# A table of 200 steps: moving the second half of the side work between attention blocks

## The chip, the core and the metric

The kernel runs on one core of a Trainium2 chip. A core has TensorE (PE in the profile, matmuls, with PEld for its weight loads), VectorE (DVE), ScalarE (ACT), GpSimd (POOL) and SyncE (SP, which here only issues transfers). The engines run side by side and wait for each other by semaphores; each works through its own list in the order in which it was built. The metric is the device time of one execution in microseconds, the median over runs.

## The reference

A hybrid encoder block on 1024 tokens of width 1024, with 16 learned meta tokens ahead of them, all in float32:

```python
u = _rms_norm(h, pre_w)
rq, rk, rv, rg, aq, ak, av, ag, gr, ga = _split_in(u @ w_in)
...                       # branch A: o_r = bidirectional retention, 4 heads, gated by silu(rg)
y_r = o_r.astype(h.dtype) @ w_rb
aq = _pad_front(_rotary(aq.reshape(B, T, ATT_HEADS, ATT_HD), pos))     # 8 heads of 128
ak = _pad_front(_rotary(ak.reshape(B, T, ATT_GROUPS, ATT_HD), pos))    # 2 groups of keys
o_a = _windowed_sink_attention(aq, ak, av, sink)[:, META_PAD:].reshape(B, T, ATT_Q)
y_a = (o_a * jax.nn.silu(ag.astype(jnp.float32))).astype(h.dtype) @ w_ab
mix = jax.nn.sigmoid(gr) * y_r + jax.nn.sigmoid(ga) * y_a
return h + _rms_norm(mix @ w_o, post_w)
```

The attention works in blocks of 128 queries. Each sees its own block of keys, the ones beside it (distance at most 128) and the 16 meta keys; a learned sink per head enters the softmax's maximum and sum.

## The kernel before

Every float32 product is made of three fp32r products: each operand is split in a high and a low half (`...h`, `...l`), and `mm3` (L72) issues high x high (L74), low x high (L75) and high x low (L76). The high half of most operands is a copy on ACT, the low half is a subtraction on DVE (`dve_lo`, L90).

The program has four stretches: the first projections and retention (0 to about 337 us), the attention (about 337 to 570), the gates' and branches' products, and the output product with its norm. The change lies in the attention.

The attention takes the 8 heads in 4 pairs, hp = 0 to 3, and each pair in 8 blocks, n = 0 to 7: 32 chunks, written (hp, n), with k as their running number. For a chunk, `stage1` makes the scores of both heads on TensorE (`ps`), masks them and takes the row minimum on DVE (`raw`, `nm`, L1369), makes exponentials and their sum on ACT (`p`, `den`, L1372), the inverse on DVE (L1375) and the scaling on POOL (L1382). `stage2` transposes p on TensorE (`pt`) and splits the result (`pah`, `pm`, `pbh` on ACT; `pal`, `pm`, `pbl` on DVE). `stage3` multiplies by the values (`po`) and copies out on ACT (`oa`, L1440).

TensorE's order is: scores of the next chunk, transposes of this one, then `fill`: some steps of other matmuls, as many as `FILL` says (5 to 10), then `stage3` of the chunk before. A step is three matmuls of 512 columns and takes about 0.7 us: such matmuls start 0.235 us apart. There are 200 steps: projections of later queries (`gen_aq`, tile `paq`) and keys (`gen_ak`, `pak`), and the first part of later gate products (`pre`, `pe`). The queries of pair 3 take steps 128 to 159. The weight units of `pre` take eight steps each from 160: unit 9 at 160, 10 at 168, 11 at 176, 12 at 184, 13 at 192.

What else those steps need, on ACT, DVE and by transfers, is begun by the table `BEGUN`: step number, then the functions that are called right after it. They are:

- `sum_fetch(q)` loads, and `sum_row(q, 0)` and `(q, 1)` scale on ACT (L726) and subtract on DVE (L729) one eighth of the sums of x (tile `xs`, two operations on ACT and four on DVE in all), which are stored for products after the attention.
- `fetch_aq(hp)` loads a query weight; `half_w('q', hp, s)` splits its half s (`wh` on ACT L116, `wl` on DVE L90, both 128x1024).
- `split_q(hp, e, i)` splits rotated queries (`aqh` on ACT L641, `aql` on DVE L90): half i of the blocks of head e of the pair. The tiles are aq_00, 01, 10, 11, with i first.
- `keys(1, i)` splits the rotated keys `akr` of piece i (`kTh` on ACT L687, `kTl` on DVE L90). The rotation itself ends in two transfers that POOL issues (L185).
- `pre_fetch(u)` loads the two halves of a gate weight (`we`, L762; the two buffers are shared with the unit before), `pre_sum(u, 0..2)` makes sums in it on DVE (L774) and `pre_parts(u)` splits it (`weh` on ACT L784, `wel` on DVE L90).

`hooked` puts what it begins behind the latest mark of the attention, and a scheduler then sets the final order of each engine's list:

```python
with follow(*marks("exp", "sum", "lo", "hi")):
    for f, *a in at.get(n, ()):
        f(*a)
```

`x_to_out` copies 1 MB of x to the output, three times, after the chunks that a tuple names. It issues on SP, as do all loads and stores here but the rotations' (POOL).

Of the kernel before, what the change touches and what calls it, by code (L numbers as in the profile page):

```python
# [38 lines left out]
def block_kernel(ctx: ExitStack, tc: tile.TileContext, x0, xT, x, meta, w_in, w_rb, w_ab, w_out, post_w,  # L39
# [39 lines left out]
    def follow(*ins):  # L79

        st = ExitStack()
        for i in ins:
            st.enter_context(tc.issue_after(i))
        return st
# [595 lines left out]
    def keys(g, i):  # L680

        if not i:
            kT[g] = [ra.tile([P, 4, 272], R, tag="kp", bufs=2, name=f"kT{s}{g}") for s in "hl"]
        kh, kl = kT[g]
        o = rotated_k.pop((g, i))
        s = NM if i == 0 else 0
        nc.scalar.copy(kh[:, i, 0:256], o[:, s:s + 256])  # L687
        dve_lo(kl[:, i, 0:256], o[:, s:s + 256], kh[:, i, 0:256])
        if i == 0:
            for j in range(4):  # L690
                nc.scalar.copy(kh[:, j, 256:272], o[:, 0:NM])
                dve_lo(kl[:, j, 256:272], o[:, 0:NM], kh[:, j, 256:272])
# [139 lines left out]
    def marks(*names):  # L832
        return [last[m] for m in names if m in last]
# [498 lines left out]
    def attention():  # L1332
# [96 lines left out]
        def stage3(hp, n):  # L1429
            g = hp // 2  # L1430
            bl, m = st2.pop((hp, n))
            po = p3(f"po{hp}_{n}")
            for j, (b, h_, l_) in enumerate(bl):
                mm3(po[:, 0:256], *(t[:, P * g:P * g + P] for t in (vah[:, b], low_value(b))), h_, l_, j == 0, False)
            latest[:] = [nc.tensor.matmul(po[:, 0:256], vm[:, P * g:P * g + P], m, start=False,
                                          stop=True).ins]
            if n % 2 == 0:
                oa[0] = ap.tile([P, 2, 256], F32, tag="oa", bufs=2, name=f"oa{hp}_{n}")
            o0 = P * (n % 2)
            last["oa"] = nc.scalar.copy(oa[0][:, :, o0:o0 + P],  # L1440
                                        po[:, 0:256].rearrange("p (e t) -> p e t", e=2)).ins
            if n % 2:
                stored.append(nc.sync.dma_start(
                    oTa_d[2 * hp:2 * hp + 2, :, P * (n - 1):P * (n + 1)].rearrange("e p t -> p e t"), oa[0]).ins)
# [13 lines left out]
        for k, (hp, n) in enumerate(chunks):  # L1458
            ends = k >= len(chunks) - 2
            if k + 1 < len(chunks):  # L1460
                with follow(*latest, *marks("oa", "lo")):
                    stage1(*chunks[k + 1])
                if chunks[k + 1] == (1, NB - 1):
                    keys(1, 0)
            if chunks[k] == (3, NB - 2):

                with follow(*latest):
                    fill(FILL[hp][n])
                yield
            if not k:  # L1470
                with follow(*latest):
                    fill(FILL[hp][n] - 3)
            with follow(*latest, *marks("exp", "sum")) if not ends else ExitStack():
                stage2(hp, n)
            if k and not ends:
                with follow(*latest):
                    fill(FILL[hp][n])
            with follow(*latest) if not ends else ExitStack():
                if k:
                    stage3(*chunks[k - 1])  # L1480
            if ends:
                yield
            if k in (12, 17, 21):
                x_to_out({12: 0, 17: 4, 21: 6}[k])
        stage3(*chunks[-1])


# [4 lines left out]
             39: [(sum_fetch, 1)], 40: [(pre_sum, 8, 0)], 41: [(pre_sum, 8, 1)], 42: [(pre_sum, 8, 2)],  # L1492
             43: [(pre_parts, 8)], 44: [(fetch_aq, 2)], 48: [(sum_row, 1, 0)], 49: [(sum_row, 1, 1)],
             52: [(sum_fetch, 2)], 53: [(half_w, 'q', 2, 0)], 58: [(half_w, 'q', 2, 1)], 60: [(fetch_ak,)],
             61: [(split_q, 1, 0, 1)], 65: [(split_q, 1, 1, 1)], 68: [(half_w, 'k', 1, 0)],
             72: [(half_w, 'k', 1, 1)], 74: [(sum_row, 2, 0)], 75: [(sum_row, 2, 1)], 78: [(sum_fetch, 3)],
             82: [(split_q, 2, 0, 0)], 88: [(sum_row, 3, 0)], 89: [(sum_row, 3, 1)], 90: [(split_q, 2, 1, 0)],
             91: [(sum_fetch, 4)], 96: [(sum_row, 4, 0)], 97: [(sum_row, 4, 1)], 99: [(sum_fetch, 5)],
             104: [(keys, 1, 1)], 105: [(fetch_aq, 3)], 107: [(sum_row, 5, 0)], 108: [(sum_row, 5, 1)],
             110: [(sum_fetch, 6)], 112: [(split_q, 2, 0, 1)], 114: [(half_w, 'q', 3, 0)],  # L1500
             116: [(half_w, 'q', 3, 1)], 118: [(pre_fetch, 9)], 121: [(sum_row, 6, 0)], 122: [(sum_row, 6, 1)],
             123: [(keys, 1, 2)], 124: [(sum_fetch, 7)], 125: [(pre_sum, 9, 0)], 128: [(pre_sum, 9, 1)],
             129: [(split_q, 2, 1, 1)], 130: [(pre_sum, 9, 2)], 133: [(pre_parts, 9)], 134: [(pre_fetch, 10)],
             136: [(keys, 1, 3)], 139: [(sum_row, 7, 0)], 140: [(sum_row, 7, 1)], 145: [(split_q, 3, 0, 0)],
             146: [(pre_sum, 10, 0)], 147: [(pre_sum, 10, 1)], 149: [(pre_sum, 10, 2)], 152: [(split_q, 3, 1, 0)],
             153: [(pre_parts, 10)], 154: [(pre_fetch, 11)], 161: [(pre_sum, 11, 0)], 162: [(pre_sum, 11, 1)],
             163: [(pre_sum, 11, 2)], 164: [(split_q, 3, 0, 1)], 167: [(pre_parts, 11)], 168: [(pre_fetch, 12)],
             169: [(split_q, 3, 1, 1)], 173: [(pre_sum, 12, 0)], 174: [(pre_sum, 12, 1)], 175: [(pre_sum, 12, 2)],
             177: [(pre_parts, 12)], 178: [(pre_fetch, 13)], 182: [(pre_sum, 13, 0)], 183: [(pre_sum, 13, 1)],
             184: [(pre_sum, 13, 2)], 187: [(pre_parts, 13)]}  # L1510

    def x_to_out(r):

        with tc.issue_after(stored[-1]):
            nc.sync.dma_start(out[P * r:P * r + 2 * P], x[P * r:P * r + 2 * P])

    del wak[:]
    i = attention()
    next(i)

# [102 lines left out]
```

## Time and profile before

| | |
|---|---|
| median of 3 runs | 1069.37 us (1068.57 to 1070.4) |
| the profiled execution | 1068.98 us |
| its span | 1067.2 us |
| granted TensorE clock, mean | 0.995 |
| busy: TensorE, DVE, ACT, POOL | 98%, 79%, 47%, 22% |

The span is what the profiler saw from the first instruction to the last; the execution's time is 1.78 us longer. Lines of the timeline give the start, the duration, the engine, the line of the kernel, the operation with output and input, a count where several are put together, and in brackets the idle time just before it with what ended it. "SPq" is a transfer's issue on SP. A list of waits gives the total, the number of times and the longest.

### The profile page before, as it was taken

The page shows a single profiled execution, that of the slowest core. Times are in us where ns is not written, and L with a number is a line of the kernel's source. Part 1 is how long each engine was busy: PE and PEld are TensorE (multiplying, and loading weights), DVE is VectorE, ACT ScalarE, POOL GpSimd, SP SyncE. Part 2 cuts the span into 40 slices and gives each one's busy share as a digit, 9 for nine tenths or more (in the row PEclk, how much of TensorE's full clock was granted, in tenths as well). Part 3 has the DMA queues.
Part 4 walks back from the last instruction along what each step waited for, and adds up shares of the span by engine and source line. Part 5 has one row for each costly group of instructions (what it writes and reads, how often), then busy time and mean ns, then how long its engine had stood idle before and what let it go on. Part 6 is the DMA issues. An engine that isn't in the chain of part 4 may idle for free.

```text
span 1067.2 us, 17268 instructions
## 1 busy us (share of the span) xinstructions
PE 1050.3 (98%) x5880; PEld 908.4 (85%) x5880; DVE 839.7 (79%) x1788; ACT 505.8 (47%) x1127; POOL 233.0 (22%) x338
## 2 busy tenths in 40 slices
PE   9999999999999999989999999999999999999997
PEld 8998999989999888977888888887888888788886
DVE  7886768758875777767768988998799799778665
ACT  5531422523424566555667544455456546334433
POOL 3345245243342432524310000000000000011032
PEclk9999999999999999989999999999999999999999
DMA  9433222242331465665548769899934756789463
GB/s 351 165 84 85 79 32 80 70 109 75 103 72 50 110 187 159 161 203 143 149 154 285 246 228 332 272 348 353 372 117 158 242 172 227 223 222 321 122 119 79
DMA packets 96760, 188.44 MB, mean 177 GB/s; under 512 B 10945, under 2 KB 35553, under 8 KB 95857
## 3 DMA queue, kind: packets, MB, share of 16 engines
q1 hardware_dynamic: 86352, 172.33, 48.0%
q0 software_dynamic: 10176, 14.73, 9.2%
q8 instruction: 46, 0.75, 0.3%
q10 hardware_dynamic: 144, 0.29, 0.1%
q14 instruction: 42, 0.34, 0.1%
HBM read 124.32 MB, written 57.68 MB: 171 GB/s over the span
## 4 chain that ended last, share of the span: by engine, by line
PE 89%; DMA 5%; DVE 3%; ACT 1%; issue 1%; DVEq 0%; POOLq 0%; POOL 0%; ACTq 0%; SPq 0%
PE bz L75 7%; PE bz L74 7%; PE bz L76 7%; PE pv L76 3%; PE pv L75 3%; PE pv L74 3%; PE ba L75 2%; PE br L74 2%; PE br L75 2%; PE ba L74 2%; PE ba L76 2%; PE br L76 2%; PE bo L75 2%; PE bo L74 2%; PE bo L76 2%; PE paq L75 2%
## 5 line engine op out<-in xcount | busy, mean ns | idle before, releaser
L1246 POOL DMA_DIRECT2D mx_d<-c1a x4 | 3.6, 890 | 402.4 <-DVE c1a L1237 383.2
L75 PE MATMUL bz<-T,llz 128*128 128x512 f32 x192 | 76.2, 397 | 0.0
L74 PE MATMUL bz<-T,lhz 128*128 128x512 f32 x192 | 75.6, 395 | 0.0
L76 PE MATMUL bz<-T,lhz 128*128 128x512 f32 x192 | 75.4, 393 | 0.0
L74 PE MATMUL pv<-wh,big 128*128 128x256 f32 x256 | 73.4, 287 | 0.0
L75 PE MATMUL pv<-wh,big 128*128 128x256 f32 x256 | 73.2, 286 | 0.0
L76 PE MATMUL pv<-wl,big 128*128 128x256 f32 x256 | 73.2, 286 | 0.0
L75 PE MATMUL bz<-big,llz 128*128 128x512 f32 x176 | 69.6, 395 | 0.2 <-DVE llz L90 0.2
L76 PE MATMUL bz<-big,lhz 128*128 128x512 f32 x176 | 69.5, 395 | 0.0
L74 PE MATMUL bz<-big,lhz 128*128 128x512 f32 x176 | 68.8, 395 | 0.2 <-ACT lhz L942 0.2
L1382 POOL TENSOR_SCALAR p<-p,den 128x400 f32<-128x400 f32 (+1 forms) x60 | 40.4, 776 | 80.6 <-DVE den L1375 73.8
L1372 ACT ACTIVATE p<-raw,nm 128x401 f32<-128x401 f32 (+1 forms) x64 | 38.2, 599 | 41.1 <-DVE nm L1369 40.9
L74 PE MATMUL paq<-big,wh 128*128 128x512 f32 x128 | 51.8, 404 | 0.0
L75 PE MATMUL paq<-big,wl 128*128 128x512 f32 x128 | 50.6, 395 | 0.0
L76 PE MATMUL paq<-big,wh 128*128 128x512 f32 x128 | 50.6, 395 | 0.0
L76 PEld LDWEIGHTS pv<-wl,big 128*128 128x128 f32 x256 | 48.3, 189 | 0.4
L74 PEld LDWEIGHTS pv<-wh,big 128*128 128x128 f32 x256 | 48.3, 188 | 0.4
L75 PEld LDWEIGHTS pv<-wh,big 128*128 128x128 f32 x256 | 48.3, 189 | 0.3
L1369 DVE CUSTOM_DVE_ANT_0 raw<-ps,mask,nsink 128x400 f32<-128x400 f32 (+1 forms) x64 | 36.3, 598 | 10.7 <-PE ps L76 10.2
L90 DVE TENSOR_TENSOR wl<-wr,wh 128x1024 fp32r<-128x1024 f32 x28 | 34.9, 1250 | 11.8 <-POOL wh L87 6.8
L74 PEld LDWEIGHTS bz<-T,lhz 128*128 128x128 f32 x192 | 36.0, 188 | 9.1 <-ACT u2z L1024 0.2
L76 PEld LDWEIGHTS bz<-T,lhz 128*128 128x128 f32 x192 | 36.0, 188 | 8.8
(616 smaller groups left out, 3613.1 us busy)
## 6 DMA issues: line engine op xcount, KB each, us to landing
wrz<-in_w_in_dram SPq DMA_DIRECT2D x32, 512.0 KB, 5.7
wr<-in_w_in_dram SPq DMA_DIRECT2D x29, 512.0 KB, 3.7
e<-e SPq DMA_DIRECT2D x40, 256.0 KB, 4.2
we<-in_w_in_dram SPq DMA_DIRECT2D x16, 512.0 KB, 4.3
tg<-tg_d SPq DMA_DIRECT2D x32, 256.0 KB, 4.7
T<-preT SPq DMA_DIRECT2D x6, 1024.0 KB, 7.9
xn<-in_x_dram SPq DMA_DIRECT2D x8, 512.0 KB, 9.2
oTr_d<-ost SPq DMA_DIRECT2D x16, 256.0 KB, 2.1
```

What stands on the lines that cost most here:

```text
L74: nc.tensor.matmul(o, ah, bh, start=first, stop=False, **kw)
L75: nc.tensor.matmul(o, al, bh, start=False, stop=False, **kw)
L76: latest[:] = [nc.tensor.matmul(o, ah, bl, start=False, stop=last, **kw).ins]
L90: return nc.vector.tensor_tensor(o, i, hi.bitcast(F32), ALU.subtract).ins
L1246: nc.gpsimd.dma_start(d, to, accum_op=ALU.add)
L1369: nc.vector.tensor_tensor_reduce(raw[e_][:, 1:1 + wid], s[:, 0:wid], mask[:, mo:mo + wid], -SCALE, nsink[:, hd:hd + 1], ALU.add, ALU.min, ...
L1372: last["exp"] = nc.scalar.activation(p[:, 0:1 + wid], raw[e_][:, 0:1 + wid], AF.Exp, scale=-1.0, bias=nm_[:, e_:e_ + 1], accum_out=den[:, ...
L1382: nc.gpsimd.tensor_scalar(pt[e_][:, 0:wid], pt[e_][:, 0:wid], den[:, e_:e_ + 1], 1.0, op0=ALU.mult, op1=ALU.mult)
```

## The change

In the second half of `BEGUN`, from step 61 on, 40-odd entries get other step numbers; which functions are called, and how often, stays. The second of the three copies of x goes from behind chunk k = 17, (2,1), to behind k = 14, (1,6). Two lines of the table stand for all:

```diff
-            if k in (12, 17, 21):
-                x_to_out({12: 0, 17: 4, 21: 6}[k])
+            if k in (12, 14, 21):
+                x_to_out({12: 0, 14: 4, 21: 6}[k])
...
-             116: [(half_w, 'q', 3, 1)], 118: [(pre_fetch, 9)], 121: [(sum_row, 6, 0)], 122: [(sum_row, 6, 1)],
-             123: [(keys, 1, 2)], 124: [(sum_fetch, 7)], 125: [(pre_sum, 9, 0)], 128: [(pre_sum, 9, 1)],
...
+             110: [(split_q, 2, 0, 1)], 116: [(keys, 1, 2)], 117: [(half_w, 'q', 3, 0)], 121: [(half_w, 'q', 3, 1)],
+             122: [(pre_fetch, 9)], 123: [(sum_row, 6, 0)], 124: [(sum_row, 6, 1)], 127: [(sum_fetch, 7)],
```

What moves, by step:

| entry | before | now |
|---|---|---|
| sum_row 2, 3, 4, 5 (first part) | 74, 88, 96, 107 | 61, 75, 88, 100 |
| sum_row 6, 7 (first part) | 121, 139 | 123, 146 |
| sum_fetch 3, 4, 5, 6, 7 | 78, 91, 99, 110, 124 | 65, 79, 92, 105, 127 |
| split_q(1,0,1), (1,1,1), (2,0,1) | 61, 65, 112 | 66, 73, 110 |
| split_q(3,1,0), (3,1,1) | 152, 169 | 153, 172 |
| fetch_aq 3; half_w q3, both halves | 105; 114, 116 | 102; 117, 121 |
| keys(1,2) | 123 | 116 |
| pre_fetch 9, 10, 11, 12, 13 | 118, 134, 154, 168, 178 | 122, 141, 158, 171, 182 |
| pre_sum 9, 10, 11, 12, 13 (first of three) | 125, 146, 161, 173, 182 | 133, 150, 166, 176, 187 |
| pre_parts 9, 10, 11, 12, 13 | 133, 153, 167, 177, 187 | 140, 157, 170, 181, 190 |

Buffer numbers at the end of a name differ between the two builds where nothing else does. The list of ACT around the first chunks of pair 2, where `kTh<-akr_2` is the key of keys(1,2) and `p_2` belongs to chunk (2,2); before:

```order
L1410 CAST pah_0_6409<-pt_2_0_6402 128x512
L1413 CAST pm_4888<-pt_2_0_6407 32x128 x2
L116 CAST wh_0_6420<-wr_0_6266 128x1024
L116 CAST wh_1_6430<-wr_1_6267 128x1024
L1440 COPY oa_6_6380<-po_7_6457 128x2x128
L1372 ACTIVATE p_2_6469,den_2_6468<-raw_6293,nm_2_6467 128x401
L1372 ACTIVATE p_2_6469,den_2_6468<-raw_6301,nm_2_6467 128x401
L1410 CAST pah_1_6496<-pt_2_1_6487 128x512
L1413 CAST pm_4889<-pt_2_1_6492 32x128 x2
L1420 CAST pbh_1_6501<-pt_2_1_6492 128x256
L726 ACTIVATE xs_6345<-xs_6345,vec 128x512
L726 ACTIVATE xs_6347<-xs_6347,vec 128x512
```

The next row of it is `kTh_6206<-akr_2_6352`. And now:

```order
L1410 CAST pah_0_6410<-pt_2_0_6403 128x512
L1413 CAST pm_4888<-pt_2_0_6408 32x128 x2
L116 CAST wh_0_6432<-wr_0_6256 128x1024
L687 CAST kTh_6206<-akr_2_6357 128x256
L1440 COPY oa_6_6381<-po_7_6452 128x2x128
L1372 ACTIVATE p_2_6464,den_2_6463<-raw_6306,nm_2_6462 128x401
L1372 ACTIVATE p_2_6464,den_2_6463<-raw_6314,nm_2_6462 128x401
L1410 CAST pah_1_6491<-pt_2_1_6482 128x512
L1413 CAST pm_4889<-pt_2_1_6487 32x128 x2
L1420 CAST pbh_1_6496<-pt_2_1_6487 128x256
L116 CAST wh_1_6506<-wr_1_6257 128x1024
```

The key stands where the second weight half stood, ahead of p_2, and that half (wh_1) behind pbh_1.

The list of DVE at the same place, with `raw_...<-ps_2` the masked scores of chunk (2,2); before:

```order
L90 TENSOR_TENSOR pal_0_6410<-pt_2_0_6402,pah_0_6409 128x512
L90 TENSOR_TENSOR pm_4888<-pt_2_0_6407,pm_4888 32x128 x2
L90 TENSOR_TENSOR wl_0_6421<-wr_0_6266,wh_0_6420 128x1024
L182 TENSOR_TENSOR m_aq_11_6448<-paq_11_6358,sr 128x512
L183 TENSOR_TENSOR aq_11_6447<-paq_11_6358,cr 128x512
L90 TENSOR_TENSOR wl_1_6431<-wr_1_6267,wh_1_6430 128x1024
L1369 ISA raw_6293,nm_2_6467<-ps_2_6470,mask,nsink 128x400
```

And now:

```order
L90 TENSOR_TENSOR pal_0_6411<-pt_2_0_6403,pah_0_6410 128x512
L90 TENSOR_TENSOR pm_4888<-pt_2_0_6408,pm_4888 32x128 x2
L90 TENSOR_TENSOR wl_0_6433<-wr_0_6256,wh_0_6432 128x1024
L90 TENSOR_TENSOR kTl_6207<-akr_2_6357,kTh_6206 128x256
L182 TENSOR_TENSOR m_aq_11_6443<-paq_11_6363,sr 128x512
L183 TENSOR_TENSOR aq_11_6442<-paq_11_6363,cr 128x512
L1369 ISA raw_6306,nm_2_6462<-ps_2_6465,mask,nsink 128x400
```

The second weight half (wl_1) has left the place ahead of the masked scores, and the key's low half (kTl) has come ahead of the rope products (m_aq, aq).

The list of DVE in pair 3, from chunk 3's scores on; `we` with the last buffer number of unit 12, `wel` the split of unit 11. Before:

```order
L90 TENSOR_TENSOR wel_7177<-we_1_6962,weh_7176 128x1024
L90 TENSOR_TENSOR aql_11_7192<-aq_11_7032,aqh_11_7191 128x512
L1369 ISA raw_6991,nm_3_7214<-ps_3_7217,mask,nsink 128x400
L1369 ISA nm_3_7214 128x1
L1369 ISA raw_6999,nm_3_7214<-ps_3_7223,mask,nsink 128x400
L1369 ISA nm_3_7214 128x1
L1375 RECIPROCAL den_3_7215<-den_3_7215 128x2
L90 TENSOR_TENSOR pal_2_7244<-pt_3_2_7234,pah_2_7243 128x512
L90 TENSOR_TENSOR pm_4888<-pt_3_2_7239,pm_4888 32x128 x2
L90 TENSOR_TENSOR pbl_2_7249<-pt_3_2_7239,pbh_2_7248 128x256
L774 TENSOR_TENSOR we_1_7185<-we_0_7184,we_1_7185 128x4x128
```

And now:

```order
L1369 ISA raw_6991,nm_3_7210<-ps_3_7219,mask,nsink 128x400
L1369 ISA nm_3_7210 128x1
L90 TENSOR_TENSOR wel_7187<-we_1_7026,weh_7186 128x1024
L1375 RECIPROCAL den_3_7211<-den_3_7211 128x2
L90 TENSOR_TENSOR pal_2_7240<-pt_3_2_7230,pah_2_7239 128x512
L90 TENSOR_TENSOR pm_4888<-pt_3_2_7235,pm_4888 32x128 x2
L90 TENSOR_TENSOR pbl_2_7245<-pt_3_2_7235,pbh_2_7244 128x256
L90 TENSOR_TENSOR aql_11_7256<-aq_11_7032,aqh_11_7255 128x512
L774 TENSOR_TENSOR we_1_7197<-we_0_7196,we_1_7197 128x4x128
L1369 ISA raw_6983,nm_4_7289<-ps_4_7292,mask,nsink 128x400
```

The split of unit 11 has gone behind the masked scores, so fewer operations lie between it and the first sum of unit 12; the other two sums of that unit have gone behind chunk 4's work.

More of the change, by code (lines that the diff above doesn't have):

```diff
@@ L1494, in block_kernel @@
              52: [(sum_fetch, 2)], 53: [(half_w, 'q', 2, 0)], 58: [(half_w, 'q', 2, 1)], 60: [(fetch_ak,)],
[L1495 to L1498, printed above, removed]
@@ L1499, in block_kernel @@
-             104: [(keys, 1, 1)], 105: [(fetch_aq, 3)], 107: [(sum_row, 5, 0)], 108: [(sum_row, 5, 1)],
-             110: [(sum_fetch, 6)], 112: [(split_q, 2, 0, 1)], 114: [(half_w, 'q', 3, 0)],
-             116: [(half_w, 'q', 3, 1)], 118: [(pre_fetch, 9)], 121: [(sum_row, 6, 0)], 122: [(sum_row, 6, 1)],
-             123: [(keys, 1, 2)], 124: [(sum_fetch, 7)], 125: [(pre_sum, 9, 0)], 128: [(pre_sum, 9, 1)],
-             129: [(split_q, 2, 1, 1)], 130: [(pre_sum, 9, 2)], 133: [(pre_parts, 9)], 134: [(pre_fetch, 10)],
@@ L1504, in block_kernel @@
[L1504 to L1508, printed above, removed]
@@ L1509, in block_kernel @@
-             177: [(pre_parts, 12)], 178: [(pre_fetch, 13)], 182: [(pre_sum, 13, 0)], 183: [(pre_sum, 13, 1)],
-             184: [(pre_sum, 13, 2)], 187: [(pre_parts, 13)]}
+             61: [(sum_row, 2, 0)], 62: [(sum_row, 2, 1)], 65: [(sum_fetch, 3)], 66: [(split_q, 1, 0, 1)],
+             68: [(half_w, 'k', 1, 0)], 72: [(half_w, 'k', 1, 1)], 73: [(split_q, 1, 1, 1)], 75: [(sum_row, 3, 0)],
+             76: [(sum_row, 3, 1)], 79: [(sum_fetch, 4)], 82: [(split_q, 2, 0, 0)], 88: [(sum_row, 4, 0)],
@@ new lines, in block_kernel @@
+             89: [(sum_row, 4, 1)], 90: [(split_q, 2, 1, 0)], 92: [(sum_fetch, 5)], 100: [(sum_row, 5, 0)],
+             101: [(sum_row, 5, 1)], 102: [(fetch_aq, 3)], 104: [(keys, 1, 1)], 105: [(sum_fetch, 6)],
+             110: [(split_q, 2, 0, 1)], 116: [(keys, 1, 2)], 117: [(half_w, 'q', 3, 0)], 121: [(half_w, 'q', 3, 1)],
+             122: [(pre_fetch, 9)], 123: [(sum_row, 6, 0)], 124: [(sum_row, 6, 1)], 127: [(sum_fetch, 7)],
+             129: [(split_q, 2, 1, 1)], 133: [(pre_sum, 9, 0)], 134: [(pre_sum, 9, 1)], 136: [(keys, 1, 3)],
@@ new lines, in block_kernel @@
+             139: [(pre_sum, 9, 2)], 140: [(pre_parts, 9)], 141: [(pre_fetch, 10)], 145: [(split_q, 3, 0, 0)],
+             146: [(sum_row, 7, 0)], 147: [(sum_row, 7, 1)], 150: [(pre_sum, 10, 0)], 152: [(pre_sum, 10, 1)],
+             153: [(split_q, 3, 1, 0)], 154: [(pre_sum, 10, 2)], 157: [(pre_parts, 10)], 158: [(pre_fetch, 11)],
+             164: [(split_q, 3, 0, 1)], 166: [(pre_sum, 11, 0)], 167: [(pre_sum, 11, 1)], 168: [(pre_sum, 11, 2)],
+             170: [(pre_parts, 11)], 171: [(pre_fetch, 12)], 172: [(split_q, 3, 1, 1)], 176: [(pre_sum, 12, 0)],
@@ L1512, in x_to_out @@
+             178: [(pre_sum, 12, 1)], 179: [(pre_sum, 12, 2)], 181: [(pre_parts, 12)], 182: [(pre_fetch, 13)],
+             187: [(pre_sum, 13, 0)], 188: [(pre_sum, 13, 1)], 189: [(pre_sum, 13, 2)], 190: [(pre_parts, 13)]}
     def x_to_out(r):
```

## The prediction

> **What bounds the kernel now.** I read the head of the profile's page first, then the list of TensorE's waits, then the timeline around the longest of them. The first two:
>
> ```profile
> span 1067.2 us, 17268 instructions
> PE 1050.3 (98%) x5880; PEld 908.4 (85%) x5880; DVE 839.7 (79%) x1788; ACT 505.8 (47%) x1127; POOL 233.0 (22%) x338
> ...
> PE ps L74 <- ACT kTh L687: 5.0, 1, 5.0
> ...
> PE ps L75 <- DVE aql L90: 1.3, 1, 1.3
> PE ps L76 <- DVE kTl L90: 0.4, 1, 0.4
> ```
>
> TensorE is busy for 98% of the span, so what it waits less comes off the time. The change takes no matmul away: it can only remove waits and lost clock, or add them. One wait is larger than all others together, 5.0 us before scores (ps) for kTh, the upper half of a key tile. The other two shown are before scores too. All three lie in the attention, where the table sets the order. The timeline from 457 us to the end of the long wait, ACT, DVE and TensorE:
>
> ```profile
> 457.38 0.72 ACT L726 ACTIVATE xs<-xs,vec 128x512 f32<-128x512 f32 x1 [2.64 <-DMA xs<-in_xT_dram]
> 458.48 0.63 DVE L1369 CUSTOM_DVE_ANT_0 raw<-ps,mask,nsink 128x400 f32<-128x400 f32 x1
> 461.32 2.00 ACT L116 CAST wh<-wr 128x1024 fp32r<-128x1024 f32 x2
> 462.40 1.23 DVE L90 TENSOR_TENSOR wl<-wr,wh 128x1024 fp32r<-128x1024 f32 x1 [0.20 <-ACT wh L116]
> 463.65 0.69 DVE L182 TENSOR_TENSOR m_aq<-paq,sr 128x512 f32<-128x512 f32 x1
> 464.86 1.21 DVE L90 TENSOR_TENSOR wl<-wr,wh 128x1024 fp32r<-128x1024 f32 x1
> 465.99 0.63 DVE L1369 CUSTOM_DVE_ANT_0 raw<-ps,mask,nsink 128x400 f32<-128x400 f32 x1
> 466.74 0.63 ACT L1372 ACTIVATE p<-raw,nm 128x401 f32<-128x401 f32 x1 [3.03 <-DVE nm L1369]
> 470.95 0.70 PE L74 MATMUL ps<-kTh,aqh 128*128 128x400 f32 x1 [5.04 <-ACT kTh L687]
> ```
>
> The key's rope transfer, and how long that tile takes to land:
>
> ```profile
> 453.53 1.14 POOL L185 DMA_DIRECT2D akr<-m_ak  x1
> DMA to landing us min/median/max: 2.3/2.8/5.6
> ```
>
> The last transfer is issued by 454.67; with the slowest landing, 5.6, the key is there at 460.3. kTh is late by the order alone: on ACT it stands behind p of block (2,2), which waits 3.03 us for masked scores (raw, nm), and those stand on DVE behind two weight splits (wl, 462.40 and 464.86) and a rope product. What the wait does to the clock, in windows (busy time and count of PE, PEld, DVE, ACT, POOL, then granted clock, DMA share, GB/s):
>
> ```profile
> 468.00:472.00 4.00, 1.05 (x3) 1.04 (x4) 3.29 (x10) 3.12 (x9) 1.41 (x3) 0.56 1.18 369
> 472.00:476.00 4.00, 4.00 (x18) 3.70 (x18) 0.42 (x1) 0.00 (x0) 0.00 (x0) 0.59 0.85 271
> 480.00:484.00 4.00, 2.37 (x16) 1.74 (x15) 3.83 (x8) 1.23 (x4) 3.64 (x5) 1.00 0.61 133
> ```
>
> After 5.04 us idle TensorE works at about half clock: it loses 4 x 0.41 in the second window and half of the 1.05 busy us before it, 2.17 us. In the third it is idle for 1.6 us and the clock stays 1.00, so a short wait costs itself alone. The Trainium skill, "TensorE: Matmul & The Clock Gate", on the clock gate, lets an idle window of some 3.4 us halve the clock and some 3.4 us of work restore it; both rows agree, and by its figure the loss would be 1.7 us, an estimate, and the sum below 0.5 us smaller.
>
> **The change part by part.** The number of instructions and DMAs stays; every cost is one of place.
>
> (1) keys(1,2) seven steps earlier, the weight splits of q3 three and five steps later, row sum 5 seven earlier. The sum's load held ACT 2.64 us at 457.38, and DVE's raw of (2,1) behind it until 458.48. In the new order nothing of the sum stands there, so raw follows its scores, by my count about 3 us earlier. On ACT kTh then follows the first wh, ahead of p, at about 459.3, or when the key lands, 460.3 at the latest; TensorE asks for it at 470.95 - 5.04 = 465.9. On DVE the second wl goes behind pbl, so raw of (2,2) follows the rope products at about 462.3 instead of 465.99. Gain: 5.04 + 2.17 = 7.21. The cover is 5 us. What is late next is aql for block 4's scores: the second wl (1.21), one masking and one block's den to pbl (2.17, below) stand ahead of it on DVE. From raw at 462.3 I count it ready at about 473.4; TensorE, without its wait, asks at about 473.5. Cost 0 to 0.5, taken 0.25.
>
> (2) The first sum of weight unit 9, and the copy of x:
>
> ```profile
> 465.99 0.61 SPq L1515 DMA_DIRECT2D out_dram<-in_x_dram  x1
> 466.71 1.56 SPq L762 DMA_DIRECT2D we<-in_w_in_dram  x1
> 476.46 0.69 DVE L774 TENSOR_TENSOR we<-we,we 128x512 f32<-128x512 f32 x1 [4.04 <-DMA we<-in_w_in_dram]
> 481.03 0.45 PE L74 MATMUL ps<-kTh,aqh 128*128 128x400 f32 x1 [0.34 <-ACT aqh L641]
> 482.76 0.45 PE L75 MATMUL ps<-kTh,aql 128*128 128x400 f32 x1 [1.29 <-DVE aql L90]
> 489.09 1.21 DVE L90 TENSOR_TENSOR wel<-we,weh 128x1024 fp32r<-128x1024 f32 x1
> 490.69 0.63 PE L76 MATMUL ps<-kTl,aqh 128*128 128x400 f32 x2 [0.42 <-DVE kTl L90]
> ```
>
> DVE stood still for 4.04 us before that sum: its load, issued right behind the 1 MB copy, took 476.46 - 466.71 = 9.7 us. What DVE does next is late, down to aql at 482.76. The sum moves from step 125 to 133 and its load from 118 to 122, so the lead grows by four steps of 0.7 us, and the copy lies some 16 us ahead of it. I put the load's landing near 472, at 477.4 if it is as slow as before, and the sum's turn at 478.1. Gain 0.34 + 1.29 = 1.63, or nothing if the load were later still.
>
> (3) keys(1,3) keeps its step and the split of unit 9 goes from 133 to 140, so the wel of 489.09 leaves the place ahead of kTl: gain 0.42. A sum of unit 9 and two rope products stand there instead; kTl is ready at about 480.5 and asked for at 480.7. Cost 0 to 0.3, taken 0.15.
>
> (4) Row sums 2 to 5 go 7 to 13 steps earlier, 6 and 7 two and seven later. Sum 2 lands in heads 1 ahead of masked scores, where DVE has this slack:
>
> ```profile
> 407.61 0.64 DVE L1369 CUSTOM_DVE_ANT_0 raw<-ps,mask,nsink 128x400 f32<-128x400 f32 x1 [1.41 <-PE ps L76]
> ```
>
> A sum is four DVE operations of about 0.4, 1.66: all but 0.25 is covered. Cost 0 to 0.25, taken 0.05. A gain there is excluded, since TensorE waits for nothing in those blocks. The sums' loads and stores move with them past others on SP's queue; the stores are read only behind the attention.
>
> (5) The copy at block (1,6) instead of (2,1) goes out at about 450, beside the rope transfers of aq and akr:
>
> ```profile
> 436.14 0.64 SPq L1515 DMA_DIRECT2D out_dram<-in_x_dram  x1
> 438.69 1.69 POOL L185 DMA_DIRECT2D akr<-m_ak  x2 [3.50 <-DVE den L1375]
> 448.19 1.68 POOL L185 DMA_DIRECT2D aq<-m_aq  x2 [0.95 <-DVE aq L183]
> ```
>
> The first copy (436.14) stands as near to transfers of akr (438.69), which landed within 5.6. By that row, the nearest, the cost is nothing; the other bound is rival A.
>
> (6) Units 11 to 13: their sums and splits come 3 to 5 steps later and their use doesn't, so the lead from the split to the use shrinks from 9 steps to 6, 7 to 3 and 5 to 2. The landing of these loads, and rows of units 10 to 13:
>
> ```profile
> DMA to landing us min/median/max: 2.7/4.2/9.7
> 516.02 0.69 DVE L774 TENSOR_TENSOR we<-we,we 128x512 f32<-128x512 f32 x1 [0.41 <-DMA we<-in_w_in_dram]
> 532.57 0.17 DVE L1375 RECIPROCAL den<-den 128x2 f32<-128x2 f32 x1 [0.99 <-ACT p L1372]
> 534.74 1.41 DVE L774 TENSOR_TENSOR we<-we,we 128x512 f32<-128x512 f32 x2
> 542.55 0.33 SPq L762 DMA_DIRECT2D we<-in_w_in_dram  x1
> 543.45 0.63 DVE L1369 CUSTOM_DVE_ANT_0 raw<-ps,mask,nsink 128x400 f32<-128x400 f32 x1 [0.93 <-PE ps L76]
> 547.81 1.41 DVE L774 TENSOR_TENSOR we<-we,we 128x512 f32<-128x512 f32 x2
> ```
>
> A unit's second load goes out when the wel of the unit before has read the buffer. Now the sum that needs it follows 547.81 - 542.55 = 5.3 us later, and waited 0.41 once. For unit 12 the new order leaves only one block's den to pbl (534.74 - 532.57 = 2.17) and aql (as long as m_aq's 0.69, less overlap) between wel and sum: 2.7 us against a landing of 4.2 and its issue. DVE waits about 1.8, its slack there is 0.93 (543.45), and masked scores and the split come about 1 late, at 545.8 for a use at about 546: 0 to 0.5. Unit 13's split is ready at 558.9 for 558.85 with one gate product behind it: 0.2 to 0.5. Taken 0.75 for both; the other bound is rival C.
>
> Sum: -7.21 - 1.63 - 0.42 + 0.25 + 0.15 + 0.05 + 0.75 = -8.06. The profiled execution took 1068.98 us (span 1067.2 and 1.78 around it), 0.39 below the median of 1069.37. 1068.98 - 8.06 = 1060.9; with the 0.39 a median of 1061.3.
>
> **The rivals.**
>
> A. The moved copy slows the rope transfers. Rows for it:
>
> ```profile
> 454.12 0.62 ACT L641 CAST aqh<-aq 128x512 fp32r<-128x512 f32 x1 [1.83 <-DMA aq<-m_aq]
> 459.07 0.62 ACT L1372 ACTIVATE p<-raw,nm 128x401 f32<-128x401 f32 x1
> 468.52 1.17 POOL L1382 TENSOR_SCALAR p<-p,den 128x400 f32<-128x400 f32 x2 [1.61 <-DVE den L1375]
> ```
>
> If aq and akr land as slowly as the load behind the copy did, 9.7 us: aq is there at 459.6, ACT stands in aqh, ahead of p in the new order, until then, and p of (2,1) starts at 460.2 where it has 459.07 now: TensorE waits 1.1 for its transposes. akr lands at 464.4; kTh is just in time, but DVE stands in kTl, raw of (2,2) comes at 466.4, and its p leaves POOL's scaling at 469.5 (468.52, the first half, and 0.4 later than now), asked for at about 467.2: 2.3 more. 3.4 given back: 1064.7. For it: aqh waited 1.83 for this transfer even without the copy. Against it: the first copy. The Trainium skill, "DMA: Bandwidth & Descriptors", on issuing engines not being separate DMA queues, says that all issuers feed the same engines, so that the ropes, issued by POOL, aren't out of the way of SP's copy: it speaks for A and gives its time. Chance 0.14.
>
> B. No change: the stall moves. The sum of unit 9 now stands on DVE ahead of key (1,3). If its load took some 4 us longer than in the slowest case of (2), DVE would stand 4, TensorE about as long, and the clock would go as at 470.95: 4 + 2.17 less of the 8.06, 1067.5. Against it: the copy has gone from its side. Chance 0.07.
>
> C. Slower: DVE and TensorE stand before units 12 and 13. If their second loads take 9.7 as at 466.71, DVE waits 9.7 - 2.7 = 7.0; less its slack of 0.93 and the lead of three steps (2.1) TensorE idles 4.0, less two steps (1.4) 4.7, and each time, over 1.6 us as that is, I take the clock's 2.17 as well: 13.0 in all, for the 0.75 booked, 1073.6. It decides from loads of about 7.6 us, where each unit costs 4.4. Against it: those loads waited for only 0.41 from 505 us on, in a stretch without copies. Chance 0.07.
>
> **How the numbers follow.** My forecast 0.72, A 0.14, B 0.07, C 0.07. What a measurement of this kernel can tell from no change is about 0.2%, 2.1 us, so the line for faster lies at 1067.2. Forecast and A are faster, B is the same, C slower; a hundredth of the first goes to slower for what I haven't seen: 0.85, 0.07, 0.08. The forecast's own range is 1059.4, with every booked cost at nothing and 0.7 for the spread of runs, to 1063.0, with each at its upper end and as much again. For 8 in 10 the top reaches past A, 1065.5, and leaves out B and C.
>
> **What would show it.** Right: no wait of ps for kTh at 466 us and no half clock there; DVE's sum of unit 9 without a DMA wait; no wel ahead of kTl; waits of at most 0.5 us for aql and kTl around 473 and 481 us; a DVE wait of 1 to 2 us for we near 541 us. Wrong: any wait of TensorE over 3 us in the attention, aqh or kTh waiting on the rope transfers (A), we on its loads for 5 us or more (B, C), or a shift of the time outside the attention.

## The result, and the profile after

The changed kernel takes 1062.57 us, the median of 9 runs (1061.57 to 1067.28), against 1069.37 (9 runs): a ratio of 0.9945, 95% interval 0.9926 to 0.9963. It is faster by 0.55%, where 0.75% was forecast. The runs lie 5.7 us apart, and the profiled execution is the slowest of them, 1067.28 us with a span of 1064.8. Its waits are therefore more than the median has, and they show what comes and goes.

The head of its page and TensorE's list of waits:

```profile
span 1064.8 us, 17292 instructions
PE 1050.5 (99%) x5880; PEld 907.5 (85%) x5880; DVE 838.2 (79%) x1788; ACT 506.3 (48%) x1127; POOL 231.6 (22%) x338
...
PE ps L75 <- DVE aql L90: 2.0, 2, 1.7
PE pt L1399 <- DVE pal L90: 1.9, 3, 1.4
```

The 5.0 us for kTh and the 0.4 for kTl are gone; in their place stand two waits for aql and three of the transposes for pal. Around the first chunks of pair 2 (timeline of ACT, DVE and TensorE):

```profile
456.84 0.62 ACT L641 CAST aqh<-aq 128x512 fp32r<-128x512 f32 x1 [6.06 <-DMA aq<-m_aq]
457.49 0.69 DVE L90 TENSOR_TENSOR aql<-aq,aqh 128x512 fp32r<-128x512 f32 x1 [5.15 <-ACT aqh L641]
458.22 0.64 DVE L1369 CUSTOM_DVE_ANT_0 raw<-ps,mask,nsink 128x400 f32<-128x400 f32 x1
462.20 0.40 ACT L687 CAST kTh<-akr 128x256 fp32r<-128x256 f32 x1
465.10 0.63 DVE L1369 CUSTOM_DVE_ANT_0 raw<-ps,mask,nsink 128x400 f32<-128x400 f32 x1
465.79 0.45 PE L74 MATMUL ps<-kTh,aqh 128*128 128x400 f32 x1
468.52 0.87 PE L1399 MATMUL pt<-ident,p 128*128 128x128 f32 x4 [1.37 <-DVE pal L90]
469.69 0.41 PE L1404 MATMUL pt<-ident,p 128*128 128x128 f32 x2 [0.29 <-DVE pbl L90]
476.23 0.45 PE L75 MATMUL ps<-kTh,aql 128*128 128x400 f32 x1 [0.26 <-DVE aql L90]
480.73 0.68 DVE L774 TENSOR_TENSOR we<-we,we 128x512 f32<-128x512 f32 x1
```

kTh is made at 462.20, ahead of p, and TensorE takes it at 465.79 without a bracket. The sum of unit 9 (480.73) waits for no load. But ACT stood 6.06 us in aqh, on the rotation's transfer of the queries, and DVE 5.15 behind it, so that the masked scores of (2,1) come no earlier than in the kernel before (458.22), and TensorE's transposes wait 1.37 and 0.29. Some 30 us later stands something new:

```profile
491.10 0.60 SPq L1514 DMA_DIRECT2D out_dram<-in_x_dram  x1
491.75 0.57 SPq L762 DMA_DIRECT2D we<-in_w_in_dram  x1
500.20 0.69 DVE L774 TENSOR_TENSOR we<-we,we 128x512 f32<-128x512 f32 x1 [2.58 <-DMA we<-in_w_in_dram]
506.90 0.39 PE L75 MATMUL ps<-kTh,aql 128*128 128x272 f32 x1 [1.74 <-DVE aql L90]
507.76 0.55 PE L1399 MATMUL pt<-ident,p 128*128 128x128 f32 x3 [0.23 <-POOL p L1382]
...
508.00:512.00 4.00, 4.00 (x14) 3.17 (x13) 1.72 (x6) 3.03 (x8) 1.23 (x4) 0.57 0.47 161
```

The third copy of x, whose place in the code the change left alone, now goes out right ahead of unit 10's second load. The load takes 8.4 us, DVE waits 2.58, aql is 1.74 late, and behind it stands a window of 4 us with a mean clock of 0.57. The units at the end wait for nothing on TensorE; unit 12's sum waits 0.92 us on DVE:

```profile
533.36 0.69 DVE L774 TENSOR_TENSOR we<-we,we 128x512 f32<-128x512 f32 x1 [0.92 <-DMA we<-in_w_in_dram]
```

Where the time went can be read off the attention's own pace. The table gives, in each profiled execution, when TensorE starts the last product of a chunk's `po` (the matmul `po<-pm`), less the same in e4 below, the calmest of these kernels, and less the difference that was there at (1,7) already:

| chunk | before | after | e2 | e6 | e8 | e11 |
|---|---|---|---|---|---|---|
| (2,0) | 0.22 | 0.71 | 0.01 | 0.00 | 0.00 | 0.46 |
| (2,1) | 7.56 | 3.24 | 0.01 | 0.91 | 1.29 | 2.95 |
| (2,2) | 9.73 | 3.76 | 0.06 | 6.97 | 1.82 | 6.17 |
| (2,5) | 10.41 | 3.73 | 0.06 | 7.10 | 1.79 | 6.14 |
| (2,6) | 9.73 | 7.36 | 2.15 | 7.04 | 1.37 | 5.44 |
| (3,4) | 9.77 | 7.37 | 2.16 | 6.99 | 1.80 | 5.43 |

The kernel before loses 9.8 us. The changed one keeps 3.7 of loss behind the late rope transfer and adds 3.6 at (2,6), behind the third copy, in this execution. The list of waits of e4 has none in the attention that is longer than 0.3 us, so its own loss is small.

### The profile page after: what moved, and what is told of

The parts are those of the page before. It is cut to its first block, busy times and chain, and to the rows that moved or that the text cites. A ratio compares the mean times of both kernels' runs of the same rounds, so it can differ in the third digit from the quotient of the medians.

```text
span 1064.8 us, 17292 instructions
## 1 busy us (share of the span) xinstructions
PE 1050.5 (99%) x5880; PEld 907.5 (85%) x5880; DVE 838.2 (79%) x1788; ACT 506.3 (48%) x1127; POOL 231.6 (22%) x338
## 4 chain that ended last, share of the span: by engine, by line
PE 91%; DMA 3%; DVE 2%; ACT 2%; issue 1%; POOL 1%; DVEq 0%; POOLq 0%; ACTq 0%; SPq 0%
PE bz L74 8%; PE bz L75 8%; PE bz L76 8%; PE pv L76 3%; PE pv L74 3%; PE pv L75 3%; PE ba L75 2%; PE br L75 2%; PE br L74 2%; PE ba L74 2%; PE ba L76 2%; PE br L76 2%; PE bo L75 2%; PE bo L74 2%; PE bo L76 2%; PE paq L75 2%
```

## The experiments

All ratios are to the kernel before on the same chip. The kernel before had medians of 1068.6 to 1069.62 us beside these runs, so medians of different experiments can differ by about 1 us for that alone; the ratios are free of it. By the ratios the changed kernel gained 5.9 us, by the medians 6.8.

**e1: the second and third copy left out.**

```diff
-            if k in (12, 14, 21):
-                x_to_out({12: 0, 14: 4, 21: 6}[k])
+            if k == 12:
+                x_to_out(0)
```

> The changed kernel with the second and third 1 MB copy of x left out (rows 512 to 1023 of the output then lack x). Theory 1, the copies collide: the aqh wait of 6.06 us on the rope transfer and the 2.58 us wait of unit 10's sum go, and with them TensorE's 1.37 + 0.29 at 468, 1.74 at 506 and the 1.7 us of half clock behind it, so 1061 us or a little less, and runs that lie within 2 us of each other where they lay 5.7 apart. Theory 2, those transfers are slow by chance, whatever stands beside them: 1062.6 us and the same spread.

1060.23 us (1059.46 to 1060.72), 0.9909 (0.9893 to 0.9925): the spread is 1.3 us. No wait over 0.25 us is left on TensorE inside the attention but the ones that every kernel has. So the two copies cost the changed kernel 2.3 us by the medians (3.8 by the ratios) and most of its spread.

**e2: only the second copy put back behind chunk (2,1).** (`14` becomes `17` in both places.)

> The changed table with the second copy back behind chunk (2,1). Theory 1: aqh waits at most 2 us and TensorE's waits at 468 us go, 1.9 us less; the load of unit 9 is slow again (9 to 10 us), but its sum comes late enough to cover it, so no new wait; the third copy still stands beside unit 10. About 1 to 2 us below the changed kernel. If the move of the copy was needed for unit 9: a wait of 2 to 4 us before its sum, and no gain. Theory 2: no difference.

1064.84 us (1061.97 to 1066.1), 0.995 (0.9933 to 0.9966): no gain. The profile is of the fastest run, 1061.97, in which unit 9's sum waits for nothing and aqh 2.02 us. What is left there is the third copy; the other runs of e2, up to 4.1 us slower, have no profile. One row, and the window behind it:

```profile
503.45 0.39 PE L75 MATMUL ps<-kTh,aql 128*128 128x272 f32 x1 [1.75 <-DVE aql L90]
...
504.00:508.00 4.00, 3.77 (x19) 3.10 (x19) 2.77 (x9) 3.06 (x8) 1.71 (x5) 1.00 0.55 182
```

This is the wait of the changed kernel to a hundredth, 1.75 against 1.74, and here the clock stayed at 1.00: it cost 2.15 us where there it cost 3.6. Where the second copy stands made no difference that these runs can tell, against the 1 to 2 us expected. It has a rope transfer beside it here too: the aq transfers at 461.6 us landed after 8.9 us at the most, but ACT waited only 0.80 for them and TensorE not at all.

**e3 and e4: copies behind the loads of row sums.** In e4 the third copy alone, in e3 the second as well. The edit is shortened; the copies that move also leave the tuple behind the chunks:

```diff
+            x_in = nc.sync.dma_start(t, xT[4 * i + k, :, NM:T].rearrange("p (j t) -> p j t", j=2)[:, :, c]).ins
+        if q in {6: 4, 7: 6}:          # e4: {7: 6}
+            with tc.issue_after(x_in):
+                nc.sync.dma_start(out[P * r:P * r + 2 * P], x[P * r:P * r + 2 * P])     # r = 4, 6
```

> The changed table with the second and third copy issued right behind the loads of row sums 6 and 7 (about 458 and 479 us), where no transfer that is waited for soon is under way. Theory 1: as without the two copies, 1061 us or a little less and a small spread. Theory 2: as the changed kernel, 1062.6. A third way: the new places hit other loads (unit 9's, the queries of pair 3), and waits of 1 to 3 us stand there.

> Only the third copy moved, to behind the loads of row sum 7; the second stays behind (1,6). Theory 1: the wait of unit 10's sum and the half clock behind it go, 3.7 us of the changed kernel's profiled execution; TensorE's 1.4 to 1.9 us at 468 stay. About 1061.5, spread about 3 us. Theory 2: 1062.6.

e3: 1060.61 us (1059.58 to 1060.96), 0.9913 (0.9896 to 0.9929). e4: 1060.13 us (1059.74 to 1062.4), 0.9914 (0.9899 to 0.993). Both do what leaving the copies out did, and both beat the changed kernel, by 2.0 and 2.4 us in the median (3.4 and 3.3 by the ratios); all runs of e3 and four of five of e4 lie below the fastest of the changed kernel. In e4, with the second copy still at 449.5 us:

```profile
453.13 0.62 ACT L641 CAST aqh<-aq 128x512 fp32r<-128x512 f32 x1 [2.21 <-DMA aq<-m_aq]
493.03 0.69 DVE L777 TENSOR_TENSOR we<-we,we 128x512 f32<-128x512 f32 x1 [0.94 <-DMA we<-in_w_in_dram]
```

aqh waits 2.21 us, not 6.06, beside the same copy, and TensorE waits nowhere near 468. The copy is not harmless there; another transfer is late. There are seven profiles with the second copy behind (1,6). The table gives how far SP's issue of the copy follows POOL's first issue of the aq transfers at 448 us, and the slowest landing of the aq transfers and of the akr transfers that follow at 452:

| profile | copy behind aq (us) | aq lands (us) | akr lands (us) |
|---|---|---|---|
| before, e1, e2, e3, e9, e11: copy elsewhere or left out | | 4.6 to 5.3 | 2.8 to 4.1 |
| e7, e10, e12 | 0.25, 0.58, 0.59 | 8.6, 9.1, 7.4 | 6.2, 6.2, 4.4 |
| after | 1.55 | 8.7 | 6.0 |
| e4, e8, e6 | 1.86, 2.38, 2.39 | 4.8, 4.8, 5.0 | 6.2, 8.3, 8.0 |

So each of the seven has a late rope transfer: aq where the copy is out before POOL has finished issuing both aq transfers, and akr in all but e12, most of all in e6 and e8, where the copy goes out 2.3 us ahead of it. In after, e4, e6 and e8 the lists of SP are alike there; the store that stands ahead of the copy takes 0.53 us to issue in after and 0.84 to 1.36 in the others, and the copy follows it. What differs is what it costs: no wait of TensorE in e4, 1.8 us in e8, 3.7 in after. No run set this order on purpose. The third copy is the steadier loss.

**e8: the third copy right behind unit 10's second load instead of right ahead of it.** (Here, too, `21` leaves the tuple.)

```diff
+            w_ld = nc.sync.dma_start(t[:, :, 0:n], w_in[gates[u], :, 4 - 4 * j:8 - 4 * j, 0:n]).ins
+        if u == 10:
+            with tc.issue_after(w_ld):
+                nc.sync.dma_start(out[P * 6:P * 8], x[P * 6:P * 8])
```

> The changed kernel with the third copy issued right behind unit 10's second load instead of right ahead of it; nothing else moves. If the load waits for the copy's packets that are queued ahead of it: the load lands in about 4 to 5 us instead of 8.4, no wait of TensorE for aql at 506, 1060 to 1061 us. If it is the sharing of the engines with whatever runs beside it: the load takes 6 to 8 us, TensorE waits about 1 us, 1061.5 to 1062.6.

1061.23 us (1059.94 to 1063.46), 0.9933 (0.9922 to 0.9945). SyncE's issues and the sum (the lines of this kernel are shifted by three):

```profile
489.37 0.36 SPq L762 DMA_DIRECT2D we<-in_w_in_dram  x1
489.78 0.60 SPq L765 DMA_DIRECT2D out_dram<-in_x_dram  x1
494.19 0.69 DVE L777 TENSOR_TENSOR we<-we,we 128x512 f32<-128x512 f32 x1 [0.49 <-DMA we<-in_w_in_dram]
```

The load is there 4.8 us after its issue, with 1 MB issued 0.4 us behind it; with the same 1 MB 0.65 us ahead of it, it took 8.4. In e4, with no copy near, it took 5.3. The other profiles agree: 8.3 to 8.5 us in e2, e7 and e12, with the copy ahead, and 4.9 to 5.2 in e1, e3 and e9, with none near. So the order of issue decides, and what comes behind costs the load nothing that shows. The time of e8 itself isn't told from the changed kernel's by these runs, since the intervals overlap: its profile has lost 1.8 us by (2,2), where kTh waited 2.65 us for akr and the masked scores and the transposes came late behind it.

**e9: e4 with the second copy behind chunk (2,1).**

> The changed table with the second copy back behind chunk (2,1) and the third behind the loads of row sum 7. The kernel with the second copy alone put back had 1064.8 us, over the changed one, against what was expected. If that was the third copy beside unit 10: 1060 to 1061 us here, a spread under 3. If it is the second copy beside unit 9's load: 1062 to 1064, with a wait of DVE for we near 475 us.

1060.75 us (1059.74 to 1063.12), 0.9925 (0.9911 to 0.994). With the third copy away, the second may stand at either place: what e2 had over 1060.7 was the third copy. In the changed table the move of the second copy is worth nothing that shows.

**e10: the kernel before with that move alone.**

> The kernel before with the second copy behind chunk (1,6), nothing else. Unit 9's load is no longer behind it, so DVE's wait of 4.04 us before its sum and TensorE's 0.34 + 1.29 go; the wait for kTh stays, with the clock, by the order of the lists (kTh behind p of (2,2)): 1066 to 1068 us. Rival, the key comes early enough once the copy has gone: 1062 or less.

1070.59 us (1068.23 to 1071.18), 1.0008 (0.9998 to 1.0019): no change, where 1066 to 1068 was expected. The profile, at 1070.55 us:

```profile
457.89 0.62 ACT L641 CAST aqh<-aq 128x512 fp32r<-128x512 f32 x1 [5.68 <-DMA aq<-m_aq]
471.57 0.70 PE L74 MATMUL ps<-kTh,aqh 128*128 128x400 f32 x1 [4.51 <-ACT kTh L687]
475.86 1.04 PE L76 MATMUL ps<-kTl,aqh 128*128 128x400 f32 x2 [2.59 <-DVE kTl L90]
```

kTh stays late by the order of the lists, as expected. What was not: DVE still waits before unit 9's sum, 2.51 us for 4.04, and kTl has come behind that sum in this kernel's list. And the copy delays the row sums. Two rows of SP, first of the kernel before and then of this one, give the loads of sum 5:

```profile
454.56 1.06 SPq L719 DMA_DIRECT2D xs<-in_xT_dram  x2
458.69 1.44 SPq L719 DMA_DIRECT2D xs<-in_xT_dram  x2
```

They need the buffers that sum 4's stores hold. Those go out at about 449.7 us in both, but here 1 us behind the copy, and land after 8.4 to 9.0 us instead of 4.8 at the most.

**e5 and e11: the kernel before with keys(1,2) and the two halves of q3's weight on their new steps.**

```diff
-             ... 114: [(half_w, 'q', 3, 0)], 116: [(half_w, 'q', 3, 1)], ... 123: [(keys, 1, 2)], ...
+             ... 116: [(keys, 1, 2)], 117: [(half_w, 'q', 3, 0)], ... 121: [(half_w, 'q', 3, 1), (sum_row, 6, 0)], ...
```

> The kernel before with three entries of the change alone: keys(1,2) from step 123 to 116 and the two halves of q3's weight from 114 and 116 to 117 and 121. Theory 1, the key's place in the lists of ACT and DVE makes the 7.2 us: TensorE's 5.04 for kTh and the half clock behind it go, the waits of the second stall (aqh 0.34, aql 1.29) stay or grow by 1 to 2 us, since unit 9's load still lands at about 476 us behind the copy: 1062 to 1065 us. Rival, the row sums' removal from ahead of the masked scores is needed as well: 1067 or more.

1064.37 us (1063.21 to 1065.88), the median of four runs, 0.9961 (0.9948 to 0.9974). A fifth, the one that was profiled, took 2090.57 us, for which nothing in the kernel accounts; it is left out, and the same edit was run again.

> The kernel before with keys(1,2) and the halves of q3 on their new steps alone, once more, since its first profile was not of an ordinary execution. The theory wants no wait of ps for kTh near 466 us, and in its place a wait for aql or aqh of 1 to 4 us behind the sum of unit 9, whose load stands behind the second copy; 1064 to 1066 us.

1063.81 us (1063.51 to 1065.49), 0.9955 (0.9939 to 0.9971).

```profile
461.05 0.41 ACT L687 CAST kTh<-akr 128x256 fp32r<-128x256 f32 x1
468.32 0.88 PE L1399 MATMUL pt<-ident,p 128*128 128x128 f32 x4 [1.37 <-DVE pal L90]
477.36 0.69 DVE L774 TENSOR_TENSOR we<-we,we 128x512 f32<-128x512 f32 x1 [2.40 <-DMA we<-in_w_in_dram]
478.70 0.46 PE L75 MATMUL ps<-kTh,aql 128*128 128x400 f32 x1 [2.86 <-DVE aql L90]
...
480.00:484.00 4.00, 4.00 (x19) 3.26 (x19) 3.24 (x9) 3.70 (x10) 1.42 (x3) 1.00 0.95 298
```

Three entries of the table, of the 51 that move (51, not the 40-odd said above), take the kTh wait away and give half of the clean gain, 4 to 5 us. The rest is eaten by what was late next: 1.37 us for pal, because row sum 5 still stands ahead of the masked scores, and 2.86 for aql behind unit 9's sum, the one that was expected.

**e6: the changed kernel with the weight units 9 to 13 on their steps of before.**

> The changed kernel with the weight units 9 to 13 (load, sums, split) back on their steps of before. On SyncE's list the third copy then stands behind both loads of unit 10. Theory 1: the wait of unit 10's sum and the half clock go; kTl waits 0.4 again behind the split of unit 9: 1060.5 to 1061.5, and a spread under 3 us. Rival, the later units were worth something by themselves (unit 9's sum against its slow load): 1063 or more.

1065.89 us (1062.99 to 1067.42), 0.997 (0.9958 to 0.9983): the rival. The third copy does stand behind both loads of unit 10 there, and no wait is left at 500 us. But:

```profile
468.48 0.35 SPq L762 DMA_DIRECT2D we<-in_w_in_dram  x1
472.87 0.85 DVE L774 TENSOR_TENSOR we<-we,we 128x512 f32<-128x512 f32 x1 [1.52 <-DMA we<-in_w_in_dram]
476.97 0.70 PE L75 MATMUL ps<-kTh,aql 128*128 128x400 f32 x1 [3.25 <-DVE aql L90]
476.00:480.00 4.00, 3.03 (x11) 2.79 (x12) 2.91 (x9) 2.00 (x6) 0.12 (x1) 0.50 0.95 299
```

The load of unit 9 lands 4.4 us after its issue, with no copy near it, and is still too late for a sum eight steps earlier: once the kTh wait is gone, TensorE comes to aql 3.25 us before it is there, and the half clock follows. The table of the attention's pace has 6.1 us of loss for it at (2,2), and 1.63 is what the same sum cost in the kernel before.

**e7: the changed kernel with all row sums on their steps of before.**

> The changed kernel with all loads and parts of row sums back on their steps of before. The key still stands ahead of p, so the 7.2 us stay away; sum 5 stands again ahead of masked scores of block (2,2), and TensorE waits 1 to 2 us for p there; the third copy still stands ahead of unit 10's second load. Theory: 1063 to 1065, 0 to 2 above the changed kernel. Rival, the sums carry the gain: 1066 or more.

1070.11 us (1068.3 to 1072.24), 1.0014 (1.0005 to 1.0022): the rival again, and slower than the kernel before. SyncE's loads of sums 5 and 6, then what waits for them:

```profile
457.31 1.43 SPq L719 DMA_DIRECT2D xs<-in_xT_dram  x2
470.39 2.59 SPq L719 DMA_DIRECT2D xs<-in_xT_dram  x2
474.68 0.72 ACT L726 ACTIVATE xs<-xs,vec 128x512 f32<-128x512 f32 x1 [3.00 <-DMA xs<-in_xT_dram]
478.80 0.45 PE L74 MATMUL ps<-kTh,aqh 128*128 128x400 f32 x1 [1.31 <-ACT aqh L641]
480.54 0.45 PE L75 MATMUL ps<-kTh,aql 128*128 128x400 f32 x1 [1.29 <-DVE aql L90]
```

The kTh wait isn't there. But the two buffers of xs pass from sum to sum, so sum 6's load can't go out before sum 5 has been stored (a row at 465.97), and ACT stands in the next sum, between the two p of a chunk, for 3.00 us. That is not all of it: against e4 this profile has lost 4.9 us by (2,1), before TensorE meets that wait, where the aq transfer is late (ACT waited 5.09 us), sum 5 stands ahead of the masked scores and the clock halves, and 8.0 by (2,2). And sum 5's load is late by the second copy, as in e10: sum 4's stores, issued at 449.31 behind the copy of 447.99, took up to 8.0 us to land.

**e12: only row sums 5, 6 and 7 on their steps of before.**

> The changed kernel with row sums 5, 6 and 7 (load and parts) on their steps of before; sums 2 to 4 stay on the new ones. If it is the sums beside pair 2's first blocks that cost (loads that come late because the sum before holds their buffer): 1068 to 1071 us, as with all sums put back. If it is sums 2 to 4 in pair 1: 1062 to 1063.

1061.62 us (1061.28 to 1063.67), 0.9935 (0.9921 to 0.9949): on the side of the second theory, and it costs nothing that these runs can tell. The loads in this kernel:

```profile
438.08 5.73 SPq L719 DMA_DIRECT2D xs<-in_xT_dram  x2
457.75 1.35 SPq L719 DMA_DIRECT2D xs<-in_xT_dram  x2
```

The first is sum 5's, 19 us earlier than in e7, because sums 2 to 4 in pair 1 have let go of the buffers earlier, ahead of the second copy; sum 6's follows at 457.75 instead of 470.39, and no sum waits for a load. So the steps that matter for pair 2 are those of sums 2 to 4 in pair 1, a pair of heads earlier, as long as the copy stands behind (1,6). Whether they would matter with the copy behind (2,1) is open: no run has the changed table with the old sums and the copy there, and in e11, with the old sums and the copy there, sum 5's load went out at 453.89.

## Why the prediction was right, and where it wasn't

It forecast 1061.3 and got 1062.57, with the interval of the ratio on one side of 1. (Its range ended at 1063.0; its own terms at their upper ends add up to 1062.9.)

(1) Right in its mechanism: the kTh wait and the half clock behind it are gone, kTh is made ahead of p, and e11 shows that three entries do it. The size was right, too: in the table the kernel before has lost 7.6 us by (2,1), for 7.21 booked. The 0.25 booked for aql is 0.26 in this execution and nothing in e4's, so that this number agrees is luck. What is late next was named, but not that the masked scores of (2,1) would stay at 458: the rope transfer came instead of the row sum. In e4, without it, they start at 454.51, earlier by more than the 3 us counted.

(2) Right, and too small. The sum of unit 9 waits for nothing. 1.63 us was the price of its stall behind the 5 us one; without that cover, putting its steps back costs 6.1 us in e6's profile. The reason given was half wrong: the lead matters, the copy's distance (e9) doesn't.

(3) Right: kTl waits for nothing; the 0.15 booked was 0.

(4) The cost was right, nothing. "A gain there is excluded, since TensorE waits for nothing in those blocks" is a step that failed: the waits are in other blocks. Sums 2 to 4 set when the loads of 5 and 6 can start (e7 against e12, 8.5 us), and with the old ones, beside the copy's new place, the rest of the change would have been lost.

(5) "The cost is nothing" was read too kindly from its row. The akr transfers behind the first copy landed after 5.2 to 5.6 us, the one ahead of it, issued at 433.4, after 2.6: the copy had doubled the time, and nobody waited. The same profile has a row that was left out: the aq transfers issued at 465.24, beside the second copy at 465.99, took 8.8 to 9.8 us. The bound was rival A, given 0.14, and its mechanism is in all seven profiles with this copy, as a late aq or a late akr; it counted on both at once. It cost 3.7 us in the changed kernel's profile, for 3.4 forecast, but by aqh alone, to which A gave 1.1 of the 3.4, so that the sums agree is luck. In the median it costs nothing that e9 against e4 can tell. The Trainium skill, "DMA: Bandwidth & Descriptors", on issuing engines not being separate DMA queues, was the argument for it, and the table of the rope transfers agrees: POOL's transfers were late beside SP's copy in each of the seven.

(6) This is the term that was mis-sized. Units 12 and 13 cost nothing for 0.75 booked: DVE waited 0.92 for 1.8, within its slack. Unit 10 was not costed at all; the nearest the text comes is rival C, which counts on "a stretch without copies" from 505 us on. The diff leaves the third copy behind chunk k = 21; the new steps move unit 10's second load to the other side of it. That cost 3.6 us in the profile and, from e4, 2.4 by the medians or 3.3 by the ratios.

The miss of 1.3 us is about what is left of two errors: 2.4 for the third copy, not foreseen, less 0.75 and some tenths of small costs that did not come. This is an estimate from medians; by the ratios the miss is 2.2 and the copy 3.3. That the forecast came as near as it did is in part this offset.

## What to carry to other kernels

When a table moves work, write out each transfer queue's order before and after and look at every pair that changed sides, also those that the diff does not name: here a large copy that nobody waits for got ahead of a load that somebody does. Then look at the other queues for what goes out within a few microseconds behind such a copy: here the rope transfers of POOL, and a store whose buffer a later load needs. Put such copies behind the load that is due next, not ahead of it (e8), or right after one whose data is due late (e3, e4). And price what a stall hides, not only the stall: the second stall here was 1.6 us behind the first and 6 us without it, and entries whose own blocks wait for nothing kept the loads of later blocks out of the copy's way.

## What the runs showed of the hardware

A transfer of 512 KB issued 0.65 us behind one of 1 MB on the same queue took 8.4 us, issued 0.4 us ahead of one 4.8, and with none near 5.3. Transfers of 128 KB from POOL's queue, too, were late beside a copy of 1 MB from SP's, by the table under e4: 7.4 to 9.1 us instead of 4.6 to 5.3.

The clock's reaction to a wait isn't set by the wait's length alone. The prediction took 1.6 us as harmless and 5 as costly, and "a short wait costs itself alone" held only in part:

| run | TensorE's wait (us) | clock behind it |
|---|---|---|
| after | 1.74 + 0.23 | 0.57 over 4 us |
| e7 | 0.62, then 1.36 | 0.50 from about 469.1 to 472.5 |
| e2 | 1.75 + 0.23 | 1.00 |
| e11 | 2.86 | 1.00 |
| e6 | 3.25 | 0.50, then 0.69 |
| e10 | 4.51, then 2.59 | 0.50, then 0.53 |

Waits of 2 us in all halved the clock twice and once did not, and 2.86 did not. The Trainium skill, "TensorE: Matmul & The Clock Gate", Part 1 on the clock gate, describes a free-running window of about 3.4 us, so that the phase decides; the table agrees with that, and so does the half clock's length, from about 508.3 to 511.6 in the changed kernel. That a wholly idle window is needed is not what the first two rows show. No run here set the phase on purpose, so this stays an inference.
